# An encoder layer on one core: the windowed attention's scores for two heads by 64 tokens and 320 keys in place of one head by 128 tokens and 384 keys

## The chip, the core and the metric

The kernel runs on one core of a Trainium2 chip. The core has a tensor engine for matrix products (TensorE; in the profile PE for the products and PEld for the loading of their fixed operand), VectorE (DVE), ScalarE (ACT), GpSimd (POOL) and SyncE (SP), which here issues nearly all transfers between the memory outside (DRAM) and the on-chip memory SBUF. Products are written to PSUM, eight banks of 512 fp32 numbers in each of 128 rows; the other engines read PSUM and write SBUF. Each engine works through its own queue in order, and semaphores make it wait for another.

The metric is the device time of one execution in microseconds (us), as the median over runs.

## What is computed

One layer of an encoder, over two sequences of 2048 tokens, model width 1024, all in fp32:

```python
h = rms_norm(x, norm_w)
proj = h @ w_in                      # q_a 512 | k_a 128 | v_a 128 | g_a 512 | q_b, k_b, v_b, g_b 512 each
# group A: 8 query heads, 2 key/value heads, head size 64; a token sees the tokens within 128 of it
sc = jnp.einsum('bqkgd,bskd->bkgqs', qb, kb) * scale       # blocks of 128 queries, 384 keys
sc = jnp.where(valid, sc, -jnp.inf)                        # |key - query| <= 128, inside the sequence
m = jnp.maximum(jnp.max(sc, axis=-1, keepdims=True), sink_f)
e = jnp.exp(sc - m)
denom = jnp.sum(e, axis=-1, keepdims=True) + jnp.exp(sink_f - m)     # a learned sink for each head
o_a = einsum('bkgqs,bskd->bqkgd', e / denom, vb) * silu(g_a)
# group B: attention over a neighbourhood in a grid of 32 x 64 tokens, with a position bias
x = x + concat([o_a, o_b]) @ w_out
y = x + (p @ w_ple) * sigmoid(x @ w_ple_gate)
```

Only group A's attention is touched by the change. Of its 384 keys a block of 128 queries needs all, but a single query sees 257, and 64 neighbouring queries together 320.

## The kernel before

TensorE multiplies fp32 numbers in a form that keeps fewer bits of them. Each operand is therefore split into a high part, rounded to that form, and the rest, and products are formed from high and high, high and rest, rest and high. A copy on ScalarE makes the high part, a subtraction on VectorE the rest.

There are three parts. The first (up to about 780 us) goes over the 2 x 16 tiles of 128 tokens: a tile is projected to q, k, v and gate of group A, and the attention of an earlier tile is done beside it. The middle part does the same for group B, the last does the output projection and the gate with fewer products by sums of blocks.

In the first part each tile has two units, kv = 0 and 1, for the two key/value heads; a unit (`unit_a`) has the four query heads of its key head. Its steps are

- `sc` (i = 0 to 3): the scores of one head, 128 queries by 128 (k1 - k0) keys, that is 384 in an inner tile and 256 in the first and last of a sequence; two products, since q is held as high part (q1) and rest (q2) with the other parts of k in the other half of the rows. `softmax` then adds the mask on VectorE, keeps the sum in the tile s and the row's maximum in mx.
- `exps`, started behind the last `sc`: the negative maximum nm with the sink, four exponentials on ScalarE, which also give the sums den, and es, the sink's own exponential. Its second piece (step `den`) adds es to den, takes the reciprocal, multiplies the normalizer rd, and GpSimd multiplies the gate by it (g2).
- `pt` (j = 0 to 2): for each block of 128 keys the four heads' probabilities are transposed by TensorE into one PSUM tile pt, 128 keys by 4 x 128 queries, and split into pr.
- `po` (j = 0 to 2): v times pr, summed over the key blocks in PSUM; `fin` adds the two halves, multiplies by the transposed gate (pgt) and stores.

What sets the order is a list by hand, PLAN_A: each entry has a place as a share of the unit, whether it belongs to this unit (1) or to the one before (0), and the step. Between the steps TensorE's queue is filled from a stream of projection products (pk, pq, pg), which `drain` and the loop over units take one by one until the planned cost of the place is reached; the cost counts the stream's products alone (215 for one of 512 columns). TensorE's order is pinned; the other engines' orders follow from the recording layer, which places each instruction by its dependencies.

PSUM is shared by name: three banks "sc" for scores, transposes pt and the gate's transposes, three "pj" for projections, two "ms". In SBUF the scores s have five buffers and p_t, with pr in the first part, three. A new tile waits until the oldest use of its buffer is done.

## Time and profile before

| | |
|---|---|
| median of 3 runs | 2494.92 us (2492.85 to 2496.4) |
| the profiled execution: time, span | 2497.78 us, 2495.8 us |
| its instructions | 39867 |
| instructions on PE, DVE, ACT, POOL | 12920, 4274, 3341, 1033 |

The span runs from the first to the last instruction of the profiled execution. The profile gives each engine's busy time; groups of instructions by line, operation and shape, with count, busy time, mean duration, and the idle time of the engine ahead of them with what ended it; and the chain of waits, which goes back from the last instruction to what released each step, and lays the work on the path end to end. Neighbouring products overlap in their durations, so a product's duration is longer than the step from its start to the next one's. A name such as `pt<-ident,s` reads: tile pt, written from ident and s.

### The profile page before, as it was taken

Reading aid. Unit: us, or ns where it says so; the run is one execution under the profiler, and the core shown is the slowest. Engines: PE = TensorE matmul, PEld = TensorE weight load, DVE = VectorE, ACT = ScalarE, POOL = GpSimd, SP = SyncE. Lnnn points to the kernel's source line nnn. Section 1 sums busy time; section 2 is a strip of 40 time slices with the busy share of each in tenths; the row PEclk is TensorE's granted clock in tenths of the full one; section 3 lists DMA queues with packets and bytes.
Section 4 is the critical chain, followed back from the end, with each engine's and each line's share of the span. In section 5 each row is a group of like instructions: output and inputs, shape, how many; then the busy total and the mean of one; then the engine's idle time right before and its main releaser. Section 6 shows DMA issues by size and latency. Waiting matters only on the chain.

```text
span 2495.8 us, 39867 instructions
## 1 busy us (share of the span) xinstructions
PE 2474.3 (99%) x12920; PEld 2088.8 (84%) x12920; DVE 1732.5 (69%) x4274; ACT 1417.1 (57%) x3341; POOL 787.9 (32%) x1033
## 2 busy tenths in 40 slices
PE   9999999999999999999999999999999999999998
PEld 7888888888888888888888888888788888888887
DVE  6777777777775666666666676776546655687776
ACT  6677667767765566665566666665664222344443
POOL 4444444445444444444444443443110000000000
PEclk9999999999999999999999999999999999999999
DMA  5432233222254465556865666666978455756765
GB/s 199 138 118 94 87 92 102 90 92 91 88 183 140 146 197 178 166 182 187 276 184 182 184 206 197 199 203 215 307 240 278 156 171 176 265 171 219 244 225 168
DMA packets 246656, 438.86 MB, mean 176 GB/s; under 512 B 31920, under 2 KB 86320, under 8 KB 241200
## 3 DMA queue, kind: packets, MB, share of 16 engines
q1 hardware_dynamic: 246160, 436.30, 54.2%
q8 instruction: 103, 1.69, 0.3%
q14 instruction: 105, 0.86, 0.1%
q10 hardware_dynamic: 288, 0.01, 0.0%
HBM read 308.28 MB, written 133.19 MB: 177 GB/s over the span
## 4 chain that ended last, share of the span: by engine, by line
PE 93%; DMA 3%; DVE 2%; ACT 1%; issue 0%; POOL 0%; SPq 0%; DVEq 0%; ACTq 0%; POOLq 0%
PE pqk L260 14%; PE pvg L260 14%; PE acca L1171 13%; PE accc L1171 10%; PE pg L260 7%; PE pq L260 7%; PE scb L260 4%; PE ptb L263 3%; PE pob L260 3%; PE sc L260 3%; PE po L260 3%; PE pk L260 3%; PE pt L263 3%; PE pple L260 3%; DMA vw<-v_d 1%; DMA ple_d<-ev 1%
## 5 line engine op out<-in xcount | busy, mean ns | idle before, releaser
L291 ACT ACTIVATE s<-s,nm 128x384 f32<-128x384 f32 (+4 forms) x512 | 307.2, 601 | 323.9 <-DVE nm L286 195.1
L260 PE MATMUL pvg<-wb,xr 128*128 128x512 f32 x1536 | 461.5, 407 | 0.1
L260 PE MATMUL pqk<-wa,xr 128*128 128x512 f32 x1536 | 442.2, 410 | 0.0
L260 PEld LDWEIGHTS pqk<-wa,xr 128*128 128x128 f32 x1536 | 266.3, 189 | 36.9
L260 PEld LDWEIGHTS pvg<-wb,xr 128*128 128x128 f32 x1536 | 267.0, 189 | 31.8 <-DVE wb L157 0.8
L356 POOL TENSOR_TENSOR xr<-stx,xr 128x512 fp32r<-128x512 f32 x188 | 241.6, 1296 | 162.2 <-ACT xr L355 154.5
L1153 ACT CAST opd<-raw 128x512 fp32r<-128x512 f32 x224 | 131.5, 618 | 269.2 <-PE acca L1171 116.2
L1154 DVE TENSOR_TENSOR opd<-raw,opd 128x512 fp32r<-128x512 f32 x224 | 146.4, 685 | 144.2 <-ACT opd L1153 144.2
L260 PE MATMUL pg<-wb,xr 128*128 128x512 f32 x768 | 231.5, 409 | 1.0 <-DVE vv L506 1.0
L260 PE MATMUL pq<-wa,xr 128*128 128x512 f32 x768 | 222.1, 402 | 1.6 <-DVE wa L157 1.5
L275 DVE CUSTOM_DVE_ANT_0 s<-scb,bias 128x288 f32<-128x288 f32 (+3 forms) x256 | 141.9, 555 | 105.0 <-PE scb L260 102.5
L142 POOL TENSOR_TENSOR yb<-vrb,power 128x8 f32<-128x8 f32 x64 | 105.4, 1646 | 252.2 <-DVE vrb L747 239.5
L1171 PE MATMUL accc<-opd,wb 128*128 128x512 f32 x768 | 177.0, 389 | 0.2 <-DVE r L1215 0.2
L1171 PE MATMUL acca<-opd,wa 128*128 128x512 f32 x768 | 175.5, 389 | 0.0
L1171 PE MATMUL acca<-opd,s 128*128 128x512 f32 x768 | 175.4, 389 | 0.0
L1171 PEld LDWEIGHTS accc<-opd,wb 128*128 128x128 f32 x768 | 144.1, 188 | 30.5 <-DVE r L1215 0.6
L1171 PEld LDWEIGHTS acca<-opd,s 128*128 128x128 f32 x768 | 144.2, 188 | 29.9
L1171 PEld LDWEIGHTS acca<-opd,wa 128*128 128x128 f32 x768 | 144.1, 188 | 29.9
L873 DVE TENSOR_TENSOR otb<-pob,otb 64x512 f32<-64x512 f32 x128 | 88.1, 689 | 113.3 <-ACT otb L872 112.3
L260 PEld LDWEIGHTS pq<-wa,xr 128*128 128x128 f32 x768 | 140.3, 190 | 25.4 <-DVE wa L157 2.4
L260 PEld LDWEIGHTS pob<-p_t,vw 128*128 128x128 f32 (+2 forms) x832 | 132.4, 189 | 29.4 <-DVE p_t L854 5.1
L260 PEld LDWEIGHTS pg<-wb,xr 128*128 128x128 f32 x768 | 137.0, 189 | 21.9 <-DVE vv L506 1.5
(159 smaller groups left out, 5123.1 us busy)
## 6 DMA issues: line engine op xcount, KB each, us to landing
stx<-x_b SPq DMA_DIRECT2D x128, 256.0 KB
vw<-v_d SPq DMA_DIRECT2D x112, 256.0 KB
stx<-x_a SPq DMA_DIRECT2D x64, 256.0 KB
stn<-x_n SPq DMA_DIRECT2D x64, 256.0 KB
v_d<-vb SPq DMA_DIRECT2D x64, 256.0 KB
ple_d<-ev SPq DMA_DIRECT2D x64, 256.0 KB
xres<-x_r SPq DMA_DIRECT2D x64, 256.0 KB
x_d<-r SPq DMA_DIRECT2D x64, 256.0 KB
```

What stands on the lines that cost most here:

```text
L142: nc.gpsimd.tensor_tensor(out=y, in0=v, in1=power.broadcast_to([128, n]), op=ALU.pow)
L260: pinned(nc.tensor.matmul(out, lhsT, rhs, start=start, stop=stop))
L263: pinned(nc.tensor.transpose(out, in_, eye))
L275: nc.vector.tensor_tensor_reduce(out=s[:, :n], in0=ps[:, :n], in1=bias, scale=1.0, scalar=-3.0e38, op0=ALU.add, op1=ALU.max, accum_out=sm[ ...
L291: ex = nc.scalar.activation(ss[i][:, :n], ss[i][:, :n], AF.Exp, bias=nm[:, i:i + 1], accum_out=den[:, i:i + 1])
L356: low.tensor_tensor(out=lo, in0=raw, in1=hi.bitcast(F32), op=ALU.subtract)
L873: nc.vector.tensor_tensor(out=ot[a:a + 64], in0=pq[a:a + 64], in1=ot[a:a + 64], op=ALU.add)
L1153: P(nc.scalar.copy(hi, v))
L1154: P(nc.vector.tensor_tensor(out=lo, in0=v, in1=hi.bitcast(F32), op=ALU.subtract))
L1171: pinned(nc.tensor.matmul(ps, w[k][:, a, c:c + 128], o[:, b], start=i in (0, 1, 4) and k == 0 and j == 0, stop=k == 3 and j == 2, skip_gro ...
```

## The change

The four heads of a unit are no longer four blocks of rows. The transposed queries are written to PSUM so that 128 neighbouring columns hold 64 tokens of one head and the same 64 tokens of another; `sc(i)` then has pair i // 2 of heads and half i % 2 of the tile's tokens, and needs 320 keys (256 or 192 at a sequence's ends). The scores of the two halves of a pair lie in one tile of 640 columns (s2, in a buffer named ev), so that the last 64 keys of the first half and the first 64 keys of the second are neighbours. `pt` transposes the block in the middle, which all queries see, then the other whole blocks, and at j = 2 both half blocks of 64 keys at once; their parts go to two quarters of a fixed tile p_rot[2], whose two other quarters were set to zero once. `po` multiplies these over all 128 rows, 256 columns at a time, so that the zeros take the place of the keys that a half doesn't see. The sinks lie by pair and half too, and the sum of den and es brings the normalizer back to rows of tokens in four pieces.

```diff
@@ -271,6 +271,7 @@
 
-    def softmax(i, ps, n, bias, sm):
+    def softmax(i, ps, n, bias, sm, s=None):
 
-        s = main.tile([128, 512], F32, tag="s", name="s", bufs=SB)
-        nc.vector.tensor_tensor_reduce(out=s[:, :n], in0=ps[:, :n], in1=bias, scale=1.0, scalar=-3.0e38,
+        if s is None:
+            s = main.tile([128, 512], F32, tag="s", name="s", bufs=SB)[:, :n]
+        nc.vector.tensor_tensor_reduce(out=s, in0=ps[:, :n], in1=bias, scale=1.0, scalar=-3.0e38,
                                        op0=ALU.add, op1=ALU.max, accum_out=sm["mx"][:, i:i + 1])
...
@@ -290,4 +291,3 @@
         for n_, i in enumerate((0, 2, 1, 3) if sink is None else range(4)):
-            ex = nc.scalar.activation(ss[i][:, :n], ss[i][:, :n], AF.Exp, bias=nm[:, i:i + 1],
-                                      accum_out=den[:, i:i + 1])
+            ex = nc.scalar.activation(ss[i], ss[i], AF.Exp, bias=nm[:, i:i + 1], accum_out=den[:, i:i + 1])
             if sink is None and n_ == 0:
@@ -299,3 +299,8 @@
             yield
-            nc.vector.tensor_tensor(out=den, in0=den, in1=es, op=ALU.add)
+            for half in range(2):
+                for e in range(2):
+                    rows = slice(64 * e, 64 * e + 64)
+                    nc.vector.tensor_tensor(out=rd[64 * half:64 * half + 64, e::2], in0=den[rows, half::2],
+                                            in1=es[rows, half::2], op=ALU.add)
+            den = rd
         nc.vector.reciprocal(out=rd, in_=den)
@@ -439,3 +444,8 @@
     snk = ap.tile([128, 2, 8], F32, tag="snk", name="snk")
-    nc.sync.dma_start(snk[:, 0, :], io["sink"].partition_broadcast(128))
+    snk_all = ap.tile([128, 8], F32, tag="snk_all", name="snk_all")
+    nc.sync.dma_start(snk_all, io["sink"].partition_broadcast(128))
+    for e in range(2):
+        rows = slice(64 * e, 64 * e + 64)
+        nc.vector.tensor_copy(snk[rows, 0].rearrange("p (a b) -> p a b", b=2),
+                              snk_all[rows, e::2].unsqueeze(2).broadcast_to([64, 4, 2]))
     nc.vector.tensor_scalar_mul(snk[:, 1, :], snk[:, 0, :], -1.0)
...
@@ -643,4 +653,6 @@
         pqt = ptile([128, 512], "ms", "pqt")
+        halves = pqt.rearrange("p (r x e q) -> p r e x q", r=2, x=2, e=2)
         for i in range(4):
-            tr(pqt[:, 128 * i:128 * i + 128], q[:, 2 * i:2 * i + 2, :].rearrange("p h d -> p (h d)"))
+            tr(halves[:, i // 2, i % 2], q[:, 2 * i:2 * i + 2, :].rearrange("p h d -> p (h d)"),
+               ident.rearrange("p (x q) -> p x q", x=2))
         q1 = [ap.tile([128, 512], F32R, tag="q1", name="q1", bufs=3) for _ in range(2)]
...
@@ -654,14 +668,20 @@
         _, gs, y = held[f]
-        k0, k1 = max(0, t - 1), min(NT, t + 2)
-        n = 128 * (k1 - k0)
-        m0 = 128 * (k0 - t + 1)
-        sm, prs, got = sm_tiles(), [], {}
+        left, right = t > 0, t < NT - 1
+        span = [(0 if left else 128 - 64 * half, 320 if right else 256 - 64 * half) for half in range(2)]
+        sm, pairs, prs, got = sm_tiles(), [], [], {}
 
         def sc(i):
+            pair, half = divmod(i, 2)
+            a, z = span[half]
+            c0, n = 128 * t - 128 + 64 * half, z - a
+            if half == 0:
+                pairs.append(ap.tile([128, 640], F32, tag="ev", name="s2", bufs=3))
+                if not right:
+                    nc.gpsimd.memset(pairs[pair][:, 256:320], 0.0)
             ps = ptile([128, 512], "sc", "sc")
             for j, q in enumerate(qs[f]):
-                mm(ps[:, :n], q[kv][:, 128 * i:128 * i + 128], ks_a[:, kv, 128 * k0:128 * k1], j == 0, j == 1)
-            softmax(i, ps, n, mask[:, m0:m0 + n], sm)
+                mm(ps[:, :n], q[kv][:, 128 * i:128 * i + 128], ks_a[:, kv, c0 + a:c0 + z], j == 0, j == 1)
+            softmax(i, ps, n, mask[:, a:z], sm, pairs[pair][:, 320 * half + a:320 * half + z])
             if i == 3:
-                got["ex"] = exps(sm, n, y[:, 11:12], gs[:, 256 * kv:256 * kv + 256],
+                got["ex"] = exps(sm, y[:, 11:12], gs[:, 256 * kv:256 * kv + 256],
                                  (snk[:, 0, 4 * kv:4 * kv + 4], snk[:, 1, 4 * kv:4 * kv + 4]))
@@ -670,11 +690,26 @@
         def pt(j):
-            if j >= k1 - k0:
-                return
-            pt = ptile([128, 4, 128], "pt", "pt")
-            for i in range(4):
-                tr(pt[:, i, :], sm["s"][i][:, 128 * j:128 * j + 128])
-            pr = main.tile([128, 2, 512], F32R, tag="p_t", name="pr", bufs=3)
-            pf = pt.rearrange("p h q -> p (h q)")
-            nc.scalar.copy(pr[:, 0], pf)
-            nc.vector.tensor_tensor(out=pr[:, 1], in0=pf, in1=pr[:, 0].bitcast(F32), op=ALU.subtract)
+            pt = ptile([128, 512], "pt", "pt")
+            r, c = slice(0, 128), slice(0, 512)
+            if j == 2:
+                r, c = slice(0 if right else 64, 128 if left else 64), slice(0, 256)
+                for pair in range(2):
+                    tr(pt[:r.stop, 128 * pair:128 * pair + 128], pairs[pair][:, 256:256 + r.stop])
+            else:
+                if j == 1:
+                    c = slice(0 if left else 256, 512 if right else 256)
+                for x in range(c.start // 128, c.stop // 128):
+                    half, pair = divmod(x, 2)
+                    col = ((128, 384), (0, 512))[j][half]
+                    tr(pt[:, 128 * x:128 * x + 128], pairs[pair][:, col:col + 128])
+            if not p_rot:
+                p_rot.extend(main.tile([128, 2, 512], F32R, tag="p_t", name="pr", bufs=3) for _ in range(3))
+                nc.gpsimd.memset(p_rot[2][64:128, :, 0:256].bitcast(F32), 0.0)
+                nc.gpsimd.memset(p_rot[2][0:64, :, 256:512].bitcast(F32), 0.0)
+            pr = p_rot[j]
+            parts = [(r, c, c)] if j < 2 else \
+                [(slice(64 * x, 64 * x + 64), c, slice(256 * x, 256 * x + 256)) for x, there in enumerate((right, left)) if there]
+            for r, c, to in parts:
+                nc.scalar.copy(pr[r, 0, to], pt[r, c])
+            for r, c, to in parts:
+                nc.vector.tensor_tensor(out=pr[r, 1, to], in0=pt[r, c], in1=pr[r, 0, to].bitcast(F32), op=ALU.subtract)
             prs.append(pr)
@@ -684,6 +719,9 @@
                 got["po"] = ptile([128, 512], "ms", "po")
-            if j < k1 - k0:
-                v = vv[:, k0 + j, kv].rearrange("p a d -> p (a d)")
+            first, second = slice(0, 256), slice(256, 512)
+            steps = ([(0, slice(0, 512))], [(-1, first)] * left + [(1, second)] * right,
+                     [(1, first)] * right + [(-1, second)] * left)[j]
+            for d, c in steps:
+                v = vv[:, t + d, kv].rearrange("p a d -> p (a d)")
                 for i in range(2):
-                    mm(got["po"], v, prs[j][:, i], j == 0 and i == 0, k0 + j == k1 - 1 and i == 1)
+                    mm(got["po"][:, c], v, prs[j][:, i, c], j == 0 and i == 0, j == 2 and i == 1 and d == steps[-1][0])
 
@@ -694,9 +732,10 @@
             ot = ap.tile([128, 2, 128], F32, tag="ot", name="ot", bufs=2)
-            ph2 = got["po"].rearrange("p (i e q) -> p e i q", e=2, q=128)
+            ph2 = got["po"].rearrange("p (x i e q) -> p e x i q", x=2, i=2, e=2)
+            oh = ot.rearrange("p i (x q) -> p x i q", x=2)
             for e in range(2):
                 a, z = 64 * e, 64 - 64 * e
-                nc.scalar.copy(ot[a:a + 64], ph2[z:z + 64, e])
+                nc.scalar.copy(oh[a:a + 64], ph2[z:z + 64, e])
             for e in range(2):
                 a = 64 * e
-                nc.vector.tensor_tensor(out=ot[a:a + 64], in0=ph2[a:a + 64, e], in1=ot[a:a + 64], op=ALU.add)
+                nc.vector.tensor_tensor(out=oh[a:a + 64], in0=ph2[a:a + 64, e], in1=oh[a:a + 64], op=ALU.add)
             nc.vector.tensor_tensor(out=ot, in0=pgt, in1=ot, op=ALU.mult)
...
@@ -951,3 +990,3 @@
             else:
-                ev = ap.tile([128, TW], F32, tag=("ev", "sq")[m // 2 % 2], name="ev", bufs=2)
+                ev = ap.tile([128, TW], F32, tag=("ev", "sq")[m // 2 % 2], name="ev", bufs=3 - m // 2 % 2)
             P(nc.scalar.copy(ev, ps))
...
```

How TensorE's and VectorE's queues change is seen at three places; each time it is the queue before, then the queue now.

TensorE, second unit of an inner tile: the scores of the last two heads (sc), between projection products of q (pq), and then the products with the values (po), which are those of the unit before.

```order
L260 MATMUL sc<-ks_a,q_3908 128x384
L260 MATMUL sc<-ks_a,q_284 128x384
L260 MATMUL pq<-wa_111,xr 128x512
L260 MATMUL sc<-ks_a,q_3908 128x384
L260 MATMUL sc<-ks_a,q_284 128x384
L260 MATMUL po<-pr,vv 128x512 x2
L260 MATMUL pq<-wa_111,xr 128x512
L260 MATMUL pq<-wa_112,xr 128x512
L260 MATMUL po<-pr,vv 128x512 x2
L260 MATMUL pq<-wa_112,xr 128x512 x2
L260 MATMUL pq<-wa_113,xr 128x512 x2
L260 MATMUL po<-pr,vv 128x512 x2
```

```order
L260 MATMUL sc<-ks_a,q_3963 128x320
L260 MATMUL sc<-ks_a,q_287 128x320
L260 MATMUL pq<-wa_111,xr 128x512
L260 MATMUL sc<-ks_a,q_3963 128x320
L260 MATMUL sc<-ks_a,q_287 128x320
L260 MATMUL po<-pr,vv 128x512 x2
L260 MATMUL pq<-wa_111,xr 128x512
L260 MATMUL pq<-wa_112,xr 128x512
L260 MATMUL po<-pr,vv 128x256 x4
L260 MATMUL pq<-wa_112,xr 128x512 x2
L260 MATMUL pq<-wa_113,xr 128x512 x2
L260 MATMUL po<-pr,vv 128x256 x4
```

The scores have 320 columns for 384; of three pairs of 512 columns the last two have become four products of 256, at the same places in the stream.

TensorE, first unit of an inner tile: the transposes of the probabilities (pt) between projection products (pk; pq starts the next projection).

```order
L260 MATMUL pk<-wx,xr 128x256 x2
L263 MATMUL pt<-ident,s 128x128 x4
L260 MATMUL pk<-wx,xr 128x256 x6
L263 MATMUL pt<-ident,s 128x128 x4
L260 MATMUL pk<-wx,xr 128x256 x6
L260 MATMUL pq<-wa_110,xr 128x512 x2
```

```order
L260 MATMUL pk<-wx,xr 128x256 x2
L263 MATMUL pt<-ident,s_3873 128x128
L263 MATMUL pt<-ident,s_3887 128x128
L263 MATMUL pt<-ident,s_3873 128x128
L263 MATMUL pt<-ident,s_3887 128x128
L260 MATMUL pk<-wx,xr 128x256 x6
L263 MATMUL pt<-ident,s_3873 128x128
L263 MATMUL pt<-ident,s_3887 128x128
L260 MATMUL pk<-wx,xr 128x256 x6
L260 MATMUL pq<-wa_110,xr 128x512 x2
```

The third group has two transposes for four; between the groups stand as many projection products as before. The rows now name the tile of each pair of heads (buffer s_ with a number, the name s2 in the code).

VectorE, first unit of an inner tile, from the sink's term (es) to the subtractions that make the rest of the probabilities (pr).

```order
L297 TENSOR_TENSOR es<-snk,nm 128x4
L560 TENSOR_TENSOR q<-pq,y 128x512
L300 TENSOR_TENSOR den<-den,es 128x4
L301 RECIPROCAL rd<-den 128x4
L302 TENSOR_SCALAR rd<-rd,y 128x4
L701 TENSOR_TENSOR ot<-po,ot 64x256 x2
L228 SCALAR_TENSOR_TENSOR pre<-pre,nw 128x512
L702 TENSOR_TENSOR ot<-pgt,ot 128x256
L315 TENSOR_TENSOR q_281<-pqt,q_2378 64x512
L679 TENSOR_TENSOR pr<-pt,pr 128x512 x3
```

```order
L297 TENSOR_TENSOR es<-snk,nm 128x4
L570 TENSOR_TENSOR q<-pq,y 128x512
L303 TENSOR_TENSOR rd<-den,es 64x2 x4
L306 RECIPROCAL rd<-rd 128x4
L740 TENSOR_TENSOR ot<-po,ot 64x2x2x64
L307 TENSOR_SCALAR rd<-rd,y 128x4
L740 TENSOR_TENSOR ot<-po,ot 64x2x2x64
L228 SCALAR_TENSOR_TENSOR pre<-pre,nw 128x512
L741 TENSOR_TENSOR ot<-pgt,ot 128x256
L320 TENSOR_TENSOR q_287<-pqt,q_2103 64x512
L714 TENSOR_TENSOR pr<-pt,pr 128x512 x2
```

The one sum of den and es is now four, of 64 rows by 2; the scaling of rd has moved between the two output sums (ot). Right behind the last row shown, the third subtraction follows as two of 64x256.

11 lines of the change are left out of this document (6 added, 5 removed).

## The prediction

> **What bounds the kernel now.** I read the head of the page first, for the engines' shares, and then one window of the first stage, where alone the change works.
>
> ```profile
> span 2495.8 us, 39867 instructions
> PE 2474.3 (99%) x12920; PEld 2088.8 (84%) x12920; DVE 1732.5 (69%) x4274; ACT 1417.1 (57%) x3341; POOL 787.9 (32%) x1033
> ```
> ```profile
> core 0: us, PE busy (x) PEld busy (x) DVE busy (x) ACT busy (x) POOL busy (x), PEclk, DMA share, GB/s
> 40.00:760.00 720.00, 716.43 (x4107) 625.38 (x4107) 556.69 (x1673) 498.56 (x1328) 325.25 (x527) 1.00 0.34 108
> ```
>
> TensorE is busy 99% of the span, and 716.43 of 720 us in the first stage, at the full granted clock. So a nanosecond taken from TensorE's queue there comes off the end, as long as no other engine takes its place; VectorE, at 556.69 of 720, is the only candidate. How long a product really occupies TensorE can't be read from its duration, since neighbours overlap. The chain of waits lays them end to end; these are pieces of it in the second unit of an inner tile, then in an outer tile (columns: start, length, work):
>
> ```profile
> 294.16 0.35 PE sc L260 x2
> ...
> 294.98 0.70 PE sc L260 x4
> ...
> 296.26 0.47 PE po L260 x2
> ...
> 299.71 0.22 PE pgt L263 x2
> 299.93 2.09 PE pq L260 x9
> 302.02 0.44 PE pt L263 x4
> ```
> ```profile
> 408.06 1.44 PE pk L260 x12
> ...
> 409.96 0.24 PE sc L260 x2
> ```
>
> Their shapes and counts stand in the groups by form (busy time, mean duration of one):
>
> ```profile
> L260 PE MATMUL pk<-wx,xr 128*128 128x256 f32 x768 | 119.3, 294 | 0.9 <-ACT wx L156 0.4 <-DVE wx L157 0.4
> L260 PE MATMUL po<-pr,vv 128*128 128x512 f32 x368 | 115.0, 393 | 0.5 <-DVE pr L679 0.5
> L263 PE MATMUL pt<-ident,s 128*128 128x128 f32 x736 | 110.3, 272 | 1.1 <-DVE ot L702 1.1
> ...
> L260 PE MATMUL sc<-ks_a,q 128*128 128x384 f32 x448 | 106.4, 338 | 0.3 <-DVE pr L679 0.3
> ...
> L260 PE MATMUL sc<-ks_a,q 128*128 128x256 f32 x64 | 11.7, 284 | 0.2 <-DVE mx L275 0.2
> ```
>
> The prices on TensorE are therefore: 512 columns 0.232 us (2.09 / 9; po 0.47 / 2), 384 columns 0.175 (0.35 / 2), 256 columns 0.12 (1.44 / 12, and 0.24 / 2 for the scores of an outer tile), a transpose 0.11 (0.44 / 4, 0.22 / 2). The three widths lie on a straight line, 0.057 us for each 128 columns. The counts give the units: 448 = 56 inner units of 8 products with 384 keys, 64 = 8 outer units (first and last tile of a sequence, two groups each) with 256.
>
> **The change, part by part.**
>
> Scores of an inner unit: still 8 products, of 320 keys for 384. 320 lies in the middle between 256 (0.12) and 384 (0.175); a product can cost no less than the first and no more than the second, so the 8 save between 0 and 0.44 us. I take the straight line, on which 512 lies too: 0.147 each, 8 x 0.028 = 0.23 us saved.
>
> Transposes of an inner unit: 12 before, 10 after, since the third group now holds two half key blocks in one. 2 x 0.11 = 0.22 us saved. The groups of four (0.44) and two (0.22) price one alike, so splitting costs nothing visible. The query transposes (pqt) stay 4 of 128 columns and only write in another order: 0.
>
> Products with the values, inner unit: 6 of 512 columns become 2 of 512 and 8 of 256, the same 3072 columns. 8 x 0.12 - 4 x 0.232 = +0.03 us. The four added instructions bring four added weight loads, which the pk row already holds, as each of its products has a load of its own.
>
> Inner unit: -0.23 - 0.22 + 0.03 = -0.42 us; 56 of them, -23.5 us.
>
> Outer unit: 4 of 8 score products go from 256 to 192 keys, on the line 0.029 us less each, -0.12 (bounds 0 and 0.48); 8 transposes stay 8; 4 products of 512 become 2 of 512 and 4 of 256, +0.02. Together -0.1; 8 of them, -0.8 us.
>
> VectorE and ScalarE must keep up with a unit that is 0.42 us shorter. Their rows in the first stage:
>
> ```profile
> L679 DVE TENSOR_TENSOR pr<-pt,pr 128x512 fp32r<-128x512 f32 x184 | 123.2, 683 | 23.4 <-ACT pr L678 23.0
> L275 DVE CUSTOM_DVE_ANT_0 s<-sc,mask 128x384 f32<-128x384 f32 x224 | 117.6, 553 | 8.1 <-PE sc L260 6.1
> L701 DVE TENSOR_TENSOR ot<-po,ot 64x256 f32<-64x256 f32 x128 | 54.0, 422 | 4.5 <-PE pq L260 1.2 <-ACT ot L698 0.7 <-PE pgt L263 0.3
> ...
> L275 DVE CUSTOM_DVE_ANT_0 s<-sc,mask 128x256 f32<-128x256 f32 x32 | 12.5, 420 | 2.4 <-PE sc L260 1.9
> ...
> L300 DVE TENSOR_TENSOR den<-den,es 128x4 f32<-128x4 f32 x64 | 11.0, 172 | 98.9 <-ACT es L298 98.9
> ```
> ```profile
> L291 ACT ACTIVATE s<-s,nm 128x384 f32<-128x384 f32 x224 | 135.2, 605 | 113.8 <-DVE nm L289 113.8
> L678 ACT CAST pr<-pt 128x512 fp32r<-128x512 f32 x184 | 107.8, 588 | 22.4 <-PE pt L263 14.2
> ...
> L698 ACT COPY ot<-po 64x256 f32<-64x256 f32 x128 | 46.1, 360 | 2.0 <-PE po L260 1.1
> ...
> L291 ACT ACTIVATE s<-s,nm 128x256 f32<-128x256 f32 x32 | 15.9, 498 | 13.2 <-DVE nm L289 13.2
> ```
>
> ScalarE per inner unit: four exponentials over 320, 4 x (605 - 498) / 2 = 0.21 us less; the third probability copy as two of 64x256, 2 x 360 - 588 = 0.13 more. Net less; at 498.56 of 720 us it is covered.
>
> VectorE per inner unit: four mask-and-maximum steps over 320, 4 x (553 - 420) / 2 = 0.27 less; the third subtraction in two halves, 2 x 422 - 683 = 0.16 more; the sum with the sinks in four small adds for one. These three further adds are a form that the trace lacks. If each had to wait for the one before, it would cost 0.17 and the gap that a dependent step shows; if not, the pace is that of neighbours which don't depend on each other:
>
> ```profile
> 294.61 0.15 DVE L495 TENSOR_SCALAR ee<-ms_a 128x1 f32<-128x1 f32 x1
> 294.67 0.55 DVE L275 CUSTOM_DVE_ANT_0 s<-sc,mask 128x384 f32<-128x384 f32 x1
> 295.14 0.08 DVE L275 DVE_READ_ACCUMULATOR2_ANT mx<- 128x1 f32 x1
> 295.14 0.15 DVE L523 TENSOR_SCALAR vr<-ms_a 128x1 f32<-128x1 f32 x1
> 295.21 0.68 DVE L583 SCALAR_TENSOR_TENSOR gs<-gs,pg 128x512 f32<-128x512 f32 x1
> ...
> 300.19 0.16 DVE L300 TENSOR_TENSOR den<-den,es 128x4 f32<-128x4 f32 x1 [1.51 <-ACT es L298]
> 300.38 0.18 DVE L301 RECIPROCAL rd<-den 128x4 f32<-128x4 f32 x1
> ```
>
> The reciprocal starts 0.19 us after the add it needs; independent small steps free the engine after 0.06 to 0.07 us (294.61 to 294.67, 295.14 to 295.21). So three more adds cost 0.2 to 0.6 us. They write different parts of one tile and read only what is ready, so I take 0.2. VectorE's net is then +0.09 us in a unit, +0.49 at the upper bound. What covers it is its idle time. The whole inner tile (two units):
>
> ```profile
> 282.14:305.25 23.11, 23.11 (x135) 20.26 (x133) 18.14 (x55) 16.27 (x44) 10.30 (x18) 1.00 0.29 92
> ```
>
> VectorE idles 23.11 - 18.14 = 4.97 us in two units. Twice 98.9 / 64 = 1.55 of that is the wait at the head of its queue for the last exponential, in which it can do nothing else: 1.87 is left, 0.93 a unit. After the change the unit is 0.42 shorter and that wait 0.21 shorter (the exponentials), so 0.72 is left against +0.09 to +0.49. The cover holds at both ends, though at the upper one only 0.23 remains, part of it the small gaps between dependent steps.
>
> Who waits for VectorE: behind the adds stand the output sums (ot), the query remainder (q), and the subtractions that free the three buffers shared by scores, transposes and the gate's transposes; next late would be the score products. Their values products come long after: pr of 293.69 is used by the po of 298.57.
>
> Once only, or a few times: two copies that lay the sinks out (VectorE, start, under 0.2 us), two clearings of the fixed p buffer and eight of 64 columns (GpSimd, busy 325.25 of 720 us), a third buffer for ev in the last part of the middle stage: costed at nothing, hidden behind TensorE's queue; without that cover under 1 us each. The DMA queues keep their transfers and order, the mask being 64 columns narrower.
>
> Sum: -23.5 - 0.8 = -24.3 us against the profiled execution's 2497.78 (span 2495.8), that is 2473.5. The median of the runs lies 2.86 below that execution, at 2494.92; taken from it, 2470.6, and I say 2471.
>
> **Rivals.**
>
> VectorE becomes late in places. For it: the small cover above, and the wait for ACT es, which stands in a fixed place and can't be moved. Against it: 0.72 us of cover for 0.09. If the adds cost the upper 0.49 and half of that shows at the score products, TensorE gives back 0.25 x 64 = 16 us: 2487.
>
> Weight loads come onto the path, so that cutting a product in two isn't free. This is the case on the other side.
>
> ```profile
> L260 PEld LDWEIGHTS pk<-wx,xr 128*128 128x128 f32 x768 | 103.0, 193 | 4.6 <-ACT wx L156 1.1 <-DVE wx L157 0.7
> ...
> L260 PEld LDWEIGHTS po<-pr,vv 128*128 128x128 f32 x368 | 67.7, 188 | 11.3 <-DVE pr L679 1.3
> ```
>
> A load of po takes 0.188 us. If the four added ones of an inner unit were not hidden, +0.75 - 0.42 = +0.33 us x 56, with two in each outer unit about +21 us in all: 2516. It decides from 0.105 us for each added load. Against it: pk pays 0.12 us for a product of 256 with its own load of 0.193, so the load runs beside the product before it. The Trainium skill has a rule for this: its page "TensorE: Matmul & The Clock Gate", Part 3 (The mechanism), says that a weight load overlaps running products only where the row group differs, and its section on LDWEIGHTS gives columns / 1.2 ns, an estimated 107 ns for 128. By that, the four loads would cost 0.43 us a unit and the whole gain would be gone, 2495. The pk row contradicts it: full row groups, and no room for an exposed load of 107 ns beside 256 columns in 120 ns.
>
> The change does nothing: the written order shows 320 keys and ten transposes, and TensorE has no idle time to swallow a saving, so only a new wait could hide it.
>
> **How the numbers follow.** The sum as worked out: 0.78 (2467 to 2475). VectorE late in places: 0.14 (2476 to 2489). Weight loads: 0.04 (2495 to 2516). No visible effect: 0.04, as likely on either side. A difference under 0.2% (5 us) can't be told from none here. Faster: 0.78 + 0.14 = 0.92; same 0.03, slower 0.05. The range must leave out 2 in 10 at most: 2465 to 2485 holds the first case with two us of the line's uncertainty below, and most of the second.
>
> **What would show it.** Right: scores of 128x320 at about 0.147 us each in the chain, 624 transposes pt instead of 736 (56 x 10 + 8 x 8), po of 128x256 at 0.12, TensorE still at 99%, and the first stage ending 24 us earlier with the later stages unmoved. Wrong: idle time of TensorE before sc or pt with VectorE as its releaser (the adds), the 256-wide po above 0.2 us (the loads), or VectorE's wait for ACT es gone, the sign that VectorE itself had become the stage's pace.

## The result, and the profile after

The changed kernel takes 2494.65 us (median of 12 runs, 2493.05 to 2498.68), the kernel before 2493.59 us (12 runs beside them, 2492.59 to 2496.54). The ratio is 1.0003, with a 95% interval of 0.9996 to 1.0011: no difference that can be told. The forecast was 2471 us, with a range of 2465 to 2485, so both were missed. All 24 us that were expected are gone.

The head of the page of the changed kernel, and its row for the window of the first stage (columns as in the prediction):

```profile
span 2493.2 us, 40576 instructions
PE 2464.4 (99%) x13048; PEld 2075.8 (83%) x13048; DVE 1751.8 (70%) x4532; ACT 1415.4 (57%) x3405; POOL 790.2 (32%) x1043
```
```profile
40.00:760.00 720.00, 707.58 (x4236) 612.87 (x4235) 574.43 (x1927) 498.46 (x1394) 328.85 (x534) 1.00 0.34 108
```

TensorE has less to do, as forecast, but in the same 720 us it is now busy for 707.58 us where it was busy for 716.43. What it saved has become waiting. The groups by form of the changed kernel in this window say at what it waits:

```profile
L260 PE MATMUL sc<-ks_a,q 128*128 128x320 f32 x448 | 100.1, 321 | 4.7 <-DVE pr L714 1.1 <-DVE mx L276 0.2
L263 PE MATMUL pt<-ident,s 128*128 128x128 f32 x600 | 95.2, 272 | 3.0 <-DVE ot L741 2.9
L260 PE MATMUL po<-pr,vv 128*128 128x256 f32 x472 | 75.9, 281 | 0.0
L260 PEld LDWEIGHTS sc<-ks_a,q 128*128 128x128 f32 x504 | 86.7, 188 | 33.3 <-DVE mx L276 15.3 <-PE sc L260 2.4 <-DVE pr L714 1.1
L303 DVE TENSOR_TENSOR rd<-den,es 64x2 f32<-64x2 f32 x252 | 40.2, 160 | 88.4 <-ACT es L298 85.8
```

The fourth row is the one to look at: the weight loads of the score products stand idle for 33.3 us, 15.3 of them for VectorE's mask-and-maximum step (mx). In the kernel before, that row reads:

```profile
L260 PEld LDWEIGHTS sc<-ks_a,q 128*128 128x128 f32 x504 | 91.9, 188 | 15.5 <-DVE mx L275 0.8 <-DVE pr L679 0.8
```

The score product now waits for the mask step because of its buffer. Scores and transposes share three buffers, so the fourth score product of a unit takes the buffer of the first, which is free once the first mask step has read it.

The place in detail. A tile has two units; the first begins among the query products (pq), the second among the gate products (pg). (The prediction calls the unit at 294 us the tile's second, and the front text's places are labelled the same way round; it is the first. No number hangs on the label.) First the kernel before, as the timeline shows VectorE, ScalarE's copy of the third group, and TensorE around the start of a first unit (columns: start, length, work, idle time ahead of it and what ended that; rows of one kind are put together with their count):

```profile
288.72 0.16 DVE L300 TENSOR_TENSOR den<-den,es 128x4 f32<-128x4 f32 x1 [1.75 <-ACT es L298]
288.91 0.18 DVE L301 RECIPROCAL rd<-den 128x4 f32<-128x4 f32 x1
...
291.96 1.27 DVE L679 TENSOR_TENSOR pr<-pt,pr 128x512 fp32r<-128x512 f32 x2
293.69 0.69 DVE L679 TENSOR_TENSOR pr<-pt,pr 128x512 fp32r<-128x512 f32 x1 [0.45 <-ACT pr L678]
294.30 0.21 DVE L493 TENSOR_SCALAR ms_a<-ssq 128x1 f32<-128x1 f32 x1
```
```profile
293.07 0.59 ACT L678 CAST pr<-pt 128x512 fp32r<-128x512 f32 x1
```
```profile
294.00 0.51 PE L260 MATMUL sc<-ks_a,q 128*128 128x384 f32 x2
...
295.75 0.51 PE L260 MATMUL sc<-ks_a,q 128*128 128x384 f32 x2
```

The same place in the changed kernel, VectorE, then ScalarE, then TensorE:

```profile
286.11 0.66 DVE L303 TENSOR_TENSOR rd<-den,es 64x2 f32<-64x2 f32 x4 [1.54 <-ACT es L298]
286.81 0.18 DVE L306 RECIPROCAL rd<-rd 128x4 f32<-128x4 f32 x1
...
290.10 2.22 DVE L714 TENSOR_TENSOR pr<-pt,pr 128x512 fp32r<-128x512 f32 x4
292.35 0.22 DVE L503 TENSOR_SCALAR ms_a<-ssq 128x1 f32<-128x1 f32 x1
...
292.85 0.49 DVE L276 CUSTOM_DVE_ANT_0 s<-sc,mask 128x320 f32<-128x320 f32 x1
```
```profile
290.15 0.62 ACT L360 CAST xr<-stx 128x512 fp32r<-128x512 f32 x1
290.67 0.76 ACT L712 CAST pr<-pt 64x256 fp32r<-64x256 f32 x2
```
```profile
291.53 0.47 PE L260 MATMUL sc<-ks_a,q 128*128 128x320 f32 x2
...
292.89 0.40 PE L260 MATMUL pq<-wa,xr 128*128 128x512 f32 x1
293.40 0.42 PE L260 MATMUL sc<-ks_a,q 128*128 128x320 f32 x1
```

Count from ScalarE's copy of the third group of keys to the first mask step, measured against the unit's first score product. In both kernels the last transpose of that group starts 1.3 us ahead of this product. Before, the copy starts 0.93 us ahead of it (294.00 - 293.07), the small steps behind the subtractions begin 0.30 us behind it (294.30), and the mask step 0.67 (the 294.67 that the prediction shows). After, the copies start 0.86 us ahead (291.53 - 290.67), the small steps begin at 0.82 (292.35) and the mask step at 1.32 (292.85), 0.65 us later. The copies' start makes 0.07 of this, the stretch from the copies to the small steps 0.45 (1.68 for 1.23), the small steps 0.13. In the 0.45, ScalarE's two half copies have 0.17 (the third subtraction starts 0.79 us behind the start of the first copy, before 0.62) and VectorE's two half subtractions 0.28 (0.89 for 0.61).

The adds lie ahead of this stretch. They take 0.51 us more (to the reciprocal 0.70 after, 0.19 before), but VectorE has idle time behind them: in 21 of the 22 regular first units it waits 0.43 to 0.45 us for ScalarE right ahead of the third subtraction, as in the next tile:

```profile
314.29 0.86 DVE L714 TENSOR_TENSOR pr<-pt,pr 64x256 fp32r<-64x256 f32 x2 [0.44 <-ACT pr L712]
```

The unit shown above is the one exception, with 0.09; there VectorE waited earlier. The mask step comes at the same place in all 22, within 0.02 us.

Against TensorE's clock: before, the first mask step ends 1.22 us behind the unit's first score product (294.67 + 0.55 - 294.00), and the fourth score product comes at 1.75, so 0.53 us to spare. After, it ends at 1.81 us (292.85 + 0.49 - 291.53) where TensorE would be ready at about 1.6 (as it is in y1c below), and the product starts at 1.87.

Where the time went over the whole stage, by units. A unit's length is the time from its first score product to the next unit's; the stage has 63 such lengths. In both traces 44 of them lie within 0.1 us of their kind's median: 22 first and 22 second units. The other 19 are the tiles at a sequence's ends and those in which steps that are done once fall.

| units | forecast | measured, after less before |
|---|---|---|
| 22 regular first units | -9.2 us (-0.42 each) | 0.0 us |
| 22 regular second units | -9.2 us (-0.42 each) | -6.5 us (-0.295 each) |
| 19 other units | -5.7 us (12 inner x 0.42, 7 outer x 0.1) | +5.3 us |

The second units gained most of what was forecast, the first units nothing, and the others lost as much as the second ones gained.

### The profile page after: what moved, and what is told of

The parts are those of the page before. It is cut to its first block, busy times and chain, and to the rows that moved or that the text cites. A ratio compares the mean times of both kernels' runs of the same rounds, so it can differ in the third digit from the quotient of the medians.

```text
span 2493.2 us, 40576 instructions
## 1 busy us (share of the span) xinstructions
PE 2464.4 (99%) x13048; PEld 2075.8 (83%) x13048; DVE 1751.8 (70%) x4532; ACT 1415.4 (57%) x3405; POOL 790.2 (32%) x1043
## 4 chain that ended last, share of the span: by engine, by line
PE 89%; DVE 4%; ACT 3%; DMA 2%; issue 1%; POOL 0%; ACTq 0%; DVEq 0%; SPq 0%; POOLq 0%
PE pqk L260 14%; PE pvg L260 14%; PE acca L1210 14%; PE accc L1210 10%; PE pg L260 7%; PE pq L260 6%; PE scb L260 4%; PE ptb L263 3%; PE pob L260 3%; PE po L260 3%; PE pple L260 3%; PE pt L263 2%; PE sc L260 2%; PE pk L260 2%; ACT pr L712 1%; DVE pr L714 1%
## 5 line engine op out<-in xcount | busy, mean ns | idle before, releaser
L292 ACT ACTIVATE s<-s,nm 128x320 f32<-128x320 f32 (+6 forms) x512 | 294.4, 576 | 315.9 <-DVE nm L287 195.4
L714 DVE TENSOR_TENSOR pr<-pt,pr 64x256 fp32r<-64x256 f32 (+2 forms) x248 | 132.7, 546 | 19.9 <-ACT pr L712 15.5
```

Source lines behind the costliest of these rows:

```text
L292: ex = nc.scalar.activation(ss[i], ss[i], AF.Exp, bias=nm[:, i:i + 1], accum_out=den[:, i:i + 1])
L714: nc.vector.tensor_tensor(out=pr[r, 1, to], in0=pt[r, c], in1=pr[r, 0, to].bitcast(F32), op=ALU.subtract)
```

## The experiments

Two theories stood at the outset. By the first, the chain of the third group of keys is too long: its transposes, ScalarE's copies (one of the next tile's x stands among them, 290.15 above), two half subtractions, the first mask step, the buffer of the fourth score product. By the second, VectorE as a whole has become late through the four adds, which push everything behind them. The columns on units give each profiled run's stage less that of the kernel before, in us.

| kernel | us, median | ratio to before (95%) | regular first | regular second | others |
|---|---|---|---|---|---|
| changed kernel | 2494.65 | 1.0003 (0.9996 to 1.0011) | 0.0 | -6.5 | +5.3 |
| x1 one add | 2489.98 | 0.9986 (0.9977 to 0.9996) | +0.3 | -8.1 | +3.0 |
| x2 third group whole | 2475.03 | 0.9924 (0.9909 to 0.9938) | -6.7 | -8.2 | -5.5 |
| x3 both | 2473.26 | 0.9915 (0.9900 to 0.9930) | -6.8 | -8.2 | -6.1 |
| x4 `den` entry in the next unit | 2491.41 | 0.9991 (0.9982 to 1.0000) | +0.2 | -7.8 | +3.9 |
| x5 copies of x later | 2503.16 | 1.0039 (1.0025 to 1.0053) | +2.0 | -0.2 | +7.5 |
| x7 copies of x before the exponentials | 2498.13 | 1.0015 (1.0005 to 1.0024) | -1.6 | -0.3 | +4.9 |
| x8 x7 with the edit of x4 | 2492.41 | 0.9994 (0.9984 to 1.0003) | -1.5 | -4.6 | +4.4 |
| y4 x2, ScalarE in halves | 2480.59 | 0.9948 (0.9933 to 0.9963) | -5.8 | -8.2 | -1.1 |
| y5 x2, VectorE in halves | 2481.74 | 0.9955 (0.9938 to 0.9971) | -8.5 | -3.9 | -1.4 |
| x10 eight adds | 2529.27 | 1.0144 (1.0129 to 1.0159) | +9.3 | +10.9 | +14.0 |
| y1 zeros in the values, first version | 2476.00 | 0.9922 (0.9907 to 0.9937) | -6.8 | -8.2 | -5.9 |
| y1b second version | 2474.43 | 0.9925 (0.9910 to 0.9939) | -6.8 | -8.2 | -6.2 |
| y1c third version | 2474.94 | 0.9924 (0.9912 to 0.9936) | -6.8 | -8.2 | -6.0 |
| y6 y1c with the edit of x4 | 2477.09 | 0.9936 (0.9922 to 0.9949) | -6.7 | -8.2 | -4.1 |

**One add for four (x1).**

```diff
-            for half in range(2):
-                for e in range(2):
...
-                    nc.vector.tensor_tensor(out=rd[64 * half:64 * half + 64, e::2], in0=den[rows, half::2],
-                                            in1=es[rows, half::2], op=ALU.add)
-            den = rd
+            nc.vector.tensor_tensor(out=den, in0=den, in1=es, op=ALU.add)
```

> Left out: the normalizers are added as one 128 x 4 step in the order of the new score rows, so each token is divided by the normalizer of another row. Everything else is the changed kernel. In its trace the four 64 x 2 adds start 0.17 us apart, so the one add takes about 0.5 us out of VectorE per unit, behind the exponential of the sinks. The theory that VectorE as a whole has become late (load): this gives back most of what was forecast, 15 to 24 us, about 2470 to 2480 us. The theory of the third group's chain (transpose, ScalarE's copies, two half subtractions, first mask step, buffer of the fourth score product): the adds stand ahead of that chain and not in it, so at most 5 us, 2490 to 2495 us.

It gained 4.7 us against the changed kernel, and the first units gained nothing. As a theory of the whole loss, VectorE's load through the adds falls. In the first units VectorE's wait ahead of the third subtraction is 0.48 us in this trace, and the mask step starts 1.33 us behind the first score product as in the changed kernel (1.32): without the three adds VectorE only waits longer for ScalarE.

**The third group whole (x2).**

```diff
-            parts = [(r, c, c)] if j < 2 else \
-                [(slice(64 * x, 64 * x + 64), c, slice(256 * x, 256 * x + 256)) for x, there in enumerate((right, left)) if there]
+            parts = [(r, c, c)]
...
-                    mm(got["po"][:, c], v, prs[j][:, i, c], ...)
+                    mm(got["po"][:, c], v, prs[j][:, i, c if j < 2 else first], ...)
```

> Left out: the zeros. The third group of keys is copied and subtracted whole, 128 x 256, one copy and one subtraction in place of two halves each, and its products take 256 columns over all rows, so the sums take in keys that the row does not see. Products and transposes have the count and size of the changed kernel. Takes about 0.4 us out of the chain from the third transpose to the first mask step. Theory of the third group's chain: 12 to 20 us faster than the changed kernel, 2475 to 2483 us, and the wait of the fourth score product for the mask step gone. Theory of load: the subtractions are 0.26 of about 0.77 us that VectorE took on per unit, so a third of the gain, about 8 us, 2487 us.

It gained 19.6 us, the upper end of what the chain of the third group would give. All three classes of units gained, the 19 others most: they went from +5.3 to -5.5.

**The `den` entry one unit later (x4), the copies of x later (x5).** x4 moves one entry of the plan:

```diff
-    (0.14, 1, "rest", 1), (0.14, 0, "po", 0),
-    (0.22, 0, "po", 1), (0.34, 0, "po", 2), (0.36, 1, "den", 0), (0.45, 0, "fin", 0), (0.46, 1, "prep", 0),
+    (0.14, 1, "rest", 1), (0.14, 0, "po", 0), (0.18, 0, "den", 0),
+    (0.22, 0, "po", 1), (0.34, 0, "po", 2), (0.45, 0, "fin", 0), (0.46, 1, "prep", 0),
```

> Nothing left out: the four adds, the reciprocal and the step behind it are issued in the next unit among the first products of that unit's values, in place of at 0.36 of their own unit's plan. VectorE's work is the same in sum. Theory of load (its place decides): 10 us or more faster than the changed kernel, below 2485 us, if the stretch they leave is the late one. Theory of the third group's chain: within 5 us of 2494.7 us.

It came out 3.2 us below the changed kernel. The edit doesn't do what was expected of it: the plan orders TensorE's queue, and on VectorE the adds and the reciprocal stayed where they were. The same place in x4:

```profile
286.15 0.66 DVE L303 TENSOR_TENSOR rd<-den,es 64x2 f32<-64x2 f32 x4 [1.54 <-ACT es L298]
```

In every regular unit the adds begin 0.22 us behind the start of the sink's exponential, in x4 as in the changed kernel. What moved is the scaling behind them (rd with y), from 1.4 to 1.5 us behind that exponential to 2.0 in the first units and 3.6 in the second, and GpSimd's product with it. So what the adds' own place is worth was not measured, here or in x8 and y6, which have the same edit. x5 moves the copies out of the key products:

```diff
-            if i in HS and early:
-                split(f + 1, HS[i], P)
...
+            if i in (3, 5) and early:
+                split(f + 1, i // 5, P)
```

> Nothing left out: ScalarE's two copies of the next tile's x are issued among the query products in place of among the key products, where one of them (0.5 us) stands between the third transpose and the half copies of the third group. Theory of the third group's chain: the fourth score product of the unit starts up to 0.3 us earlier in 29 units, 8 us faster than the changed kernel, about 2487 us. Theory of load: VectorE's work is the same, no change, 2493 to 2496 us.

It was 8.5 us slower than the changed kernel where the chain theory had it 8 faster. ScalarE's copy between the transposes and the half copies is thus not what holds the chain: without it the half copies start only 0.07 us sooner, since they then wait for the transposes (shown under x7). Instead the regular second units lost all their gain, and the first ones 0.09 us each, at the transposes near their end. What went wrong ahead of the second units is to be seen on VectorE and GpSimd, first VectorE, then GpSimd:

```profile
301.48 0.97 DVE L307 TENSOR_SCALAR rd<-rd,y 128x4 f32<-128x4 f32 x1
```
```profile
301.13 1.30 POOL L361 TENSOR_TENSOR xr<-stx,xr 128x512 fp32r<-128x512 f32 x1 [0.52 <-ACT xr L360]
```

GpSimd's subtraction, which follows each copy of x, now runs while VectorE scales the normalizers. That step of 4 columns takes 0.97 us and ends at 302.45, where GpSimd's ends at 302.43. In the changed kernel it takes 211 ns in the mean (groups by form from 60 to 320 us):

```profile
L307 DVE TENSOR_SCALAR rd<-rd,y 128x4 f32<-128x4 f32 x23 | 4.9, 211 | 0.0
```

**Both edits (x3).** The diffs of x1 and x2 together.

> Both edits of the one-add kernel and of the whole-third kernel, and it leaves out what they leave out. Alone they gave 4.7 and 19.6 us against the changed kernel. If the adds and the halves lengthen one and the same stretch, taking both away gives little beyond the 19.6 us, 2472 to 2475 us, since the stretch is then shorter than TensorE's part of it. If they are separate losses the gains add up: 24.3 us, about 2470 us, the forecast.

2473.26 us, 21.4 below the changed kernel: not the sum of 24.3, but little more than the whole third alone (1.8 us below x2), and inside the 2472 to 2475 that stood for one shared stretch. The two gains overlap: in the second units one add alone brings -8.1 us, the whole third alone -8.2 and both -8.2, and in the first units only the whole third brings anything. Once the halves are gone, the three adds are within TensorE's work.

**The copies of x before the exponentials (x7), and with the edit of x4 (x8).** As x5, with the products 1 and 2 in place of 3 and 5; x8 has the edit of x4 as well.

> Nothing left out: ScalarE's two copies of the next tile's x are issued behind the second and third query product, before the unit's exponentials, so that neither stands in front of the two copies of the results that the earlier trial delayed. Theory that ScalarE's copy alone holds the third group: 8 us faster than the changed kernel, 2487 us. Theory of two equal bounds (VectorE stands back to back behind the four adds up to the first mask step, with 0.09 us of idle time): the copy's place is worth no more than that 0.09 us in 29 units, 2 to 3 us, 2492 us.

> Nothing left out: ScalarE's two copies of the next tile's x before the exponentials, and the four adds in the next unit. Theory of two equal bounds: the two together give more than the sum of the two alone (3.2 us for the adds' place and what the copies' place gives by itself), 8 to 14 us faster than the changed kernel, 2481 to 2487 us. If each edit's effect stands by itself: 5 us faster, 2490 us.

Both missed. x7 was 3.5 us slower than the changed kernel, though the first units gained 1.6 us, 0.07 each. The expectation takes VectorE for the second bound, from the unit shown above. But in 20 of the 22 regular first units VectorE still waits 0.36 to 0.38 us ahead of the third subtraction. The second bound is TensorE's transposes, for which ScalarE's half copies now wait:

```profile
290.64 0.76 ACT L712 CAST pr<-pt 64x256 fp32r<-64x256 f32 x2 [0.35 <-PE pt L263]
```

The second units again lost their gain. Here it is the negated maximum (nm) that meets GpSimd, again VectorE first:

```profile
295.13 0.46 DVE L290 SCALAR_TENSOR_TENSOR nm<-mx,snk 128x4 f32<-128x4 f32 x1
```
```profile
294.96 0.61 POOL L322 CAST q<-q 64x512 fp32r<-64x512 f32 x1
```

It takes 0.46 us for its usual 0.16, and ends at 295.59, GpSimd's copy at 295.57. The exponentials wait for nm, the adds for the exponentials, so the whole stretch starts later. x8 won 2.2 us in place of 8 to 14. It couldn't test its theory, since its edit left the adds in place; its first units gain 1.5 us, what x7's do, and its chain is the same, from the transposes through the halves.

**Which halves (y4, y5).** Both start from x2 and cut one engine's work on the third group in two halves of 64 rows again:

```diff
-            for r, c, to in parts:
+            for r, c, to in parts if j < 2 or not (left and right) else [(slice(64 * x, 64 * x + 64), c, c) for x in range(2)]:
                 nc.scalar.copy(pr[r, 0, to], pt[r, c])
```

(y4; y5 has the same line ahead of VectorE's subtraction.)

> The whole-third kernel, and it leaves out the zeros as that one does, but ScalarE copies the third group in two halves of 64 rows again; VectorE subtracts it whole. The copies of the changed kernel start 0.39 us apart, so ScalarE is 0.39 us longer in the chain ahead of the subtraction. If the third group's loss of 19.6 us lies with ScalarE's halves: 12 us or more slower than the whole-third kernel, 2487 us or above. If it lies with VectorE's halves: under 6 us, 2475 to 2481 us. If each half adds its length to one chain, both this kernel and the next come out between, near 2485 us.

> The whole-third kernel, and it leaves out the zeros as that one does, but VectorE subtracts the third group in two halves of 64 rows again; ScalarE copies it whole. The half subtractions of the changed kernel start 0.43 us apart, where the whole one lets the next step start 0.34 us behind it, so VectorE is some 0.5 us longer. If the loss lies with VectorE's halves: 12 us or more slower than the whole-third kernel, 2487 us or above. If it lies with ScalarE's: under 6 us, 2475 to 2481 us. If both are in one chain: near 2485 us.

ScalarE's halves alone cost 5.6 us against x2, VectorE's alone 6.7; together, in the changed kernel, 19.6. So neither engine is the cause by itself. Each used up room, and the loss is more than the sum once the room is gone. The first units show it directly (medians): the first mask step ends 1.53 us behind the unit's first score product in x2, 1.56 in y4, 1.44 in y5 and 1.81 in the changed kernel, and TensorE reaches the fourth score product at 1.59. Against x2 the regular units of y4 lose 0.9 us and the others 4.5; in y5 the second units lose 4.3 and the others 4.1, while the first gain 1.8. In the first units of y5 VectorE does the gate's step (gs, 0.68 us) behind the first mask step and in x2 ahead of it; the mask step starts at 0.94 us for 1.04, and the second product of the fourth score 0.09 us sooner. Of y4's 4.5 us in the other units 2.7 lie in a single one, in which a transfer comes late (see the units at the ends, below).

**Eight adds (x10).** `for half in range(2)` becomes `for half in (0, 1, 0, 1)`.

> Nothing left out: the changed kernel with the four adds issued twice, so VectorE has four more adds of 64 x 2 per unit, 0.17 us apart, 0.68 us. If VectorE between the adds and the mask steps has no room left (it stands back to back there in one unit of two, with 0.37 us of idle time in the other), nearly all of it goes into the time: 0.3 us in one unit and 0.6 us in the other, 29 of each, 20 to 28 us slower than the changed kernel, 2515 to 2523 us. If the adds are covered, as the forecast had it, 2495 to 2500 us.

It was 34.6 us slower than the changed kernel, more than either figure: 34.6 / 64 = 0.54 us per unit for 0.68 to 0.8 us of VectorE. Its VectorE at the start of a first unit, and the weight loads of its score products:

```profile
298.96 1.46 DVE L303 TENSOR_TENSOR rd<-den,es 64x2 f32<-64x2 f32 x8 [1.78 <-ACT es L298]
...
306.10 0.49 DVE L276 CUSTOM_DVE_ANT_0 s<-sc,mask 128x320 f32<-128x320 f32 x1
```
```profile
304.35 0.53 PE L260 MATMUL sc<-ks_a,q 128*128 128x320 f32 x2
```
```profile
L260 PEld LDWEIGHTS sc<-ks_a,q 128*128 128x128 f32 x480 | 80.1, 190 | 66.8 <-PE sc L260 23.8 <-DVE mx L276 16.1 <-issue 11.4
```

Eight adds take 1.46 us, so the price of one is the same, 0.17 to 0.18. The first mask step now ends 2.24 us behind the first score product (306.59 - 304.35), 0.43 later than in the changed kernel. In the first units 0.43 of the 0.80 us come through and the rest goes into VectorE's wait ahead of the third subtraction, which is gone. So four adds were covered there, and eight are not.

**The zeros in the values (y1, y1b, y1c).** The gain of x2 with nothing left out. GpSimd copies one half of the values' rows into buffers whose other half stays zero; the third group of probabilities can then be copied and subtracted whole:

```diff
+            for x in range(2):
+                P(nc.gpsimd.tensor_copy(zeros[(f + 4) % 5][64 * x:64 * x + 64, x], vv[64 * x:64 * x + 64, t]))
...
-                v = vv[:, t + d, kv].rearrange("p a d -> p (a d)")
+                v = (vv[:, t + d, kv] if j < 2 else zeros[(f + d + 4) % 5][:, int(d < 0), kv]).rearrange("p a d -> p (a d)")
```

In y1 and y1b four such buffers rotate in place of five. There the values of the last two tiles, which are projected as a pair, take the place of values that are still to be used, so two tiles of the second sequence are computed with other values; the instructions are the same. The five of y1c leave nothing out.

> Nothing left out: the zeros are moved from the scores to the values. GpSimd makes, once a tile, two copies of the values with one half of the rows zero; the third group is copied and subtracted whole, 128 x 256, and its products of 256 columns over all rows take those values. TensorE, ScalarE and VectorE do what they do in the whole-third kernel; GpSimd has two copies of 64 x 256 more per tile, some 0.5 us each by its 64 x 512 copies of 0.61 to 0.95 us. The chain theory: as the whole-third kernel, 2474 to 2479 us, faster than the kernel before by 0.6 to 0.8%. If the gain of the whole-third kernel came from something that it left out: near 2494 us.

> The kernel with the zeros moved to the values, with nothing left out: the four buffers of those values are used in another order, so that the last tile's are still there when the second stage takes buffers of that kind. Its work is that of the first version, which ran in 2476.0 us, so 2472 to 2479 us, 0.6 to 0.9% faster than the kernel before, if the chain of the third group is the cause.

> The kernel with the zeros in the values and five buffers of such values in place of four; nothing is left out. TensorE, ScalarE and VectorE do what they do in the whole-third kernel. If the halves of 64 rows are the cause and the zeros themselves cost nothing: 2472 to 2478 us, 0.9905 to 0.994 of the kernel before. If the early gain hung on the values that were overwritten: nearer to 2494 us.

2476.00, 2474.43 and 2474.94 us. The last is 0.9924 of the kernel before (0.9912 to 0.9936), the best version with the whole computation, and it has nearly the time of x2. So the zeros cost nothing in themselves, and the halves of 64 rows do. Product by product, 21 of the regular first units of the changed kernel differ from those of y1c at one place only: the fourth score product starts 1.88 us behind the first for 1.59. Its page, and the place shown above, on VectorE, ScalarE and TensorE:

```profile
span 2473.8 us, 40452 instructions
PE 2453.1 (99%) x13048; PEld 2073.6 (84%) x13048; DVE 1730.6 (70%) x4476; ACT 1391.0 (56%) x3349; POOL 817.2 (33%) x1116
```
```profile
285.86 1.75 DVE L720 TENSOR_TENSOR pr<-pt,pr 128x512 fp32r<-128x512 f32 x3
287.52 0.20 DVE L503 TENSOR_SCALAR ms_a<-ssq 128x1 f32<-128x1 f32 x1
...
288.68 0.48 DVE L276 CUSTOM_DVE_ANT_0 s<-sc,mask 128x320 f32<-128x320 f32 x1
```
```profile
286.77 0.38 ACT L718 CAST pr<-pt 128x256 fp32r<-128x256 f32 x1
```
```profile
287.63 0.47 PE L260 MATMUL sc<-ks_a,q 128*128 128x320 f32 x2
...
289.23 0.56 PE L260 MATMUL sc<-ks_a,q 128*128 128x320 f32 x2
```
```profile
L260 PEld LDWEIGHTS sc<-ks_a,q 128*128 128x128 f32 x512 | 88.0, 188 | 20.3 <-DVE mx L276 7.1 <-DVE pr L720 0.6
L525 POOL CAST vz<-vv 64x256 fp32r<-64x256 f32 x60 | 23.7, 395 | 2.6 <-DVE vv L516 0.8
```

The three subtractions are over 1.66 us after they began (287.52 - 285.86), where the changed kernel's took 2.25. The first mask step ends at 289.16, 1.53 us behind the first score product, and the fourth score product follows at 1.60. The idle time of the weight loads is down from 33.3 to 20.3 us; GpSimd pays for it with 60 copies of 395 ns.

**The `den` entry later, with the zeros in the values (y6).** The edit of x4 on y1c.

> The same with the four adds in the next unit; nothing is left out. With the third group whole, TensorE waits 0.1 us per pair of units for the mask step. If the adds still lie in the stretch that sets it: up to 3 us faster than the kernel with the zeros in the values. If that stretch is covered now: within 1.5 us of it.

2477.09 us, 2.2 us above y1c, with intervals that overlap. The adds stay in place here too, and moving the scaling behind them gains nothing.

## Why the prediction was wrong, point by point

**TensorE's prices: right.** In the trace, score products of 320 keys start about 147 ns apart (taken: 0.147), transposes 109 ns (0.11), value products of 256 columns 117 to 120 ns (0.12). The regular second units of x1, x2 and y1c show what this is worth once nothing else is in the way: 0.37 us of the 0.42. The added weight loads cost nothing, so that rival falls, and with it the rule that was weighed there, as the pk row had it.

**The four adds: wrong within their own bounds.** Three more were taken at 0.2 us, with bounds of 0.2 and 0.6. They cost 0.51. The argument that they write different parts of one tile and read only what is ready was beside the point: they start on different rows. The gap from one to the next is 13 to 14 ns in the trace, so each waits for the one before to end. The Trainium skill has this, in its page "VectorE: DVE Perf Modes", section "Two Vector instructions with no wait between them": an instruction whose input or output starts in another group of 32 partitions than the last one's starts only when all earlier ones have finished. By that rule each of the three adds pays its whole duration, an estimated 3 x 0.172 us with the duration of the den row, 0.52; the trace agrees. The price was wrong, but it isn't what the time was lost by: in 64 units 0.51 us would be 33 us, and one add in place of four brings 4.7 (x1), nothing of it in the first units.

**The third subtraction in halves: too cheap.** It was put at +0.16 us from durations. Durations were the wrong measure, since neighbours of 128 rows overlap and halves don't: from its start to the next step's it costs 0.28 (0.89 less 0.61). VectorE's net was therefore about +0.5 us per unit in place of +0.09.

**The cover: the step that failed.** "After the change the unit is 0.42 shorter and that wait 0.21 shorter, so 0.72 is left" sets VectorE's work against its idle time averaged over two whole units, and ScalarE, too, was taken as covered from its share, "at 498.56 of 720 us". What counted was one chain across both engines, from the transposes of the third group to the first mask step. There the half copies put in 0.17 us and the half subtractions 0.28; with 0.07 at its start and 0.13 in the small steps behind, the mask step starts 0.65 us later and, being shorter, ends 0.59 later (1.81 for 1.22), while TensorE arrives 0.15 us sooner (1.60 for 1.75). The spare 0.53 us before became a wait of about 0.27 (0.21, and 0.06 from the mask step's end to the product). VectorE's idle time was there, 0.44 us of it within this very stretch, but it is the wait for ScalarE's copies: the adds ahead of it are covered by it, the halves behind it are not. Of the 0.27 us saved on the four mask steps, three quarters lie behind the chain's end, where they help nothing. y1c shows the halves to be the cause with nothing left out, y4 and y5 that it takes both engines' halves.

**What would be late next: right in the place, not in the cause.** The prediction names the score products and the three shared buffers, and the sign that would show it (idle time of TensorE ahead of sc with VectorE as its releaser). Its rival "VectorE becomes late in places" comes nearest, but it puts the loss on the adds, half of 0.49 us in 64 units, 16 us given back, and x1 gives back 4.7. Some 23 were lost (9.2 in the first units, 2.7 in the second, 11.0 in the others), and its range of 2476 to 2489 ended too early.

**The units at the ends and the steps done once: not in the sum.** The 19 other units lost 5.3 us where 5.7 were to be gained, nearly half of the miss. In x2 and y1c they gain 5.5 and 6.0 us. Four of the 19 make up 8.1 of the 10.9 us between the changed kernel and x2, and two causes can be seen there.

In the two units of one tile (from 565 us, +1.75 and +0.74 us) the order on GpSimd is another: a step for group B that is done once (rs_b, 2.9 us) runs behind a step of 0.86 us and no longer ahead of it. VectorE's next step (hr_b) waits for it with the adds queued behind, first the changed kernel, then the kernel before:

```profile
574.30 0.20 DVE L647 TENSOR_SCALAR hr_b<-rs_b 128x16 f32<-128x16 f32 x1 [3.83 <-POOL rs_b L142]
```
```profile
575.15 0.18 DVE L637 TENSOR_SCALAR hr_b<-rs_b 128x16 f32<-128x16 f32 x1 [2.01 <-POOL rs_b L142]
```

In x2 and y1c the wait is 2.01 us as before.

In another unit (from 351 us) ScalarE waits 4.6 us for a transfer (stn), in the kernel before as in the changed one, and TensorE stands 2.1 us behind it in the first and 2.7 in the second. In x2 and y1c that wait isn't there, and the unit is 2.87 us shorter than before, where 0.42 was forecast. So some 2.4 us of the gain of x2 and y1c are luck: they belong to a wait that the sum knew nothing of. Why the transfer is in time there was not followed.

What stays open: by which wait x4 gains its 3.2 us, what the adds' own place is worth, the losses in the rest of the 19 units, and the part of the first units' 0.42 us that y1c doesn't reach either (it gains 0.31). Products over 64 rows without any zeros were not tried.

## What to carry to other kernels

Idle time averaged over a unit is no cover, and idle time that is itself a wait for another engine covers only work that stands ahead of it. Find the wait that the shortened engine will meet first, follow its chain back to a point that can't move, and count only what the change adds or saves between the two. Price steps on half of the rows one behind the other, on VectorE and on ScalarE, and when a layout needs zeros, put them where the padded operand is made off the chain. A moved step takes its followers with it: here the copy of x was cheap on ScalarE, and the GpSimd subtraction behind it held up VectorE. An entry moved in a plan need not move on the other engines: look in the trace where it went before reading its time. And look at every unit of a kind before taking one as the example.

## What the runs showed of the hardware that was not expected

Steps of 64 rows that start on other rows than the one before don't overlap: adds of 64 x 2 follow each other every 0.17 us, and half subtractions of 64 x 256 every 0.43, where a whole one of 128 x 256 lets the next step begin after 0.34. On ScalarE two half copies take 0.76 us, the whole copy 0.38, and the next step begins 0.27 us after it starts.

A VectorE step of 4 columns can last as long as a GpSimd instruction that began before it: 0.97 us for 0.21 in x5, 0.46 for 0.16 in x7, with ends 16 to 28 ns behind the end of a GpSimd instruction in each of the units where it occurs (27 in x5, 27 in x7). The Trainium skill's page "SBUF — State Buffer", section "SBUF: two separate sides", has the two engines share a pair of ports that is locked for a whole instruction; these ends agree with that.
